# Loading the duplicated keys of an attention head with two 64-row transfers in place of one transfer with a repeat dimension

## The chip, the cores and the metric

The kernel runs on one core of a Trainium2 chip. The metric is device time in microseconds for one execution, the median of several. Five engines work side by side and meet at semaphores: TensorE (PE in the profile, with PEld for its weight loads), VectorE (DVE), ScalarE (ACT), GpSimd (POOL) and SyncE (SP). In this kernel every transfer is issued by SP, in program order, and carried out by the core's 16 DMA engines.

## What is computed

One inference step of a two-layer encoder over 1024 prompt positions and 8 x 16 sample positions (1152 rows of width 1024). Layer A has sliding-window attention with 16 heads on 4 key/value heads, layer B attention over the own chunk and 8 chunks back with 16 heads. After each attention come an output projection with layer norm and a GEGLU feed-forward part of width 2816 with a short causal convolution. Cut to what matters here:

```
h = x * (1 + sc_m) + sh_m
q, k, v = ...                                   # projections of h (layer B: k, v from the end of layer A)
s = einsum(q, k) * ATTN_SCALE + bias            # inside the band of chunks, else -1e30
p = softmax(s)                                  # layer A: with a learned sink per head
mix = (p @ v) @ w_o
x = layer_norm(ALPHA * x + (1 + g_m) * mix)
f = conv_ffn(x * (1 + sc_f) + sh_f)
x = layer_norm(ALPHA * x + (1 + g_f) * f)
```

All is float32. The kernel keeps that precision by writing each operand as the sum of two float32r numbers, a high part and a rest, and adding the products high x high, high x rest and rest x high.

## The kernel before

`attention(l, wk)` runs once for each layer (l is 0 and 1). First the keys and values are projected: `kproj` (L287) multiplies weights with the hidden rows `H` (through `mmT`, L266) and writes keys, split in high part and rest, to the DRAM tensor `kH[l]` (store on L299); `vproj` (L312, through `mmX`, L278) does the same for values into `vH[l]` (store on L328). Both take their staging tiles from a ring of four (`kvt`), so a tile's store must have landed before the fourth block after it can be written. In layer 1, `rescale` is woven in: for each of 9 row blocks it loads a block of `zd` (L893), multiplies and adds on POOL (L747, L748) and stores it to `xd` (L749), in a ring of two buffers.

Then 16 heads (8 pairs of channels c, two halves a) go through the prompt's attention. `kload(c, a)` brings a head's keys and values back into SBUF, into the tile `x1att`, with three transfers:

- `khi[a]` (L433), 128 partitions x 1024: the 64 rows of the high part of the keys, twice, in partitions 0 to 63 and again in 64 to 127. The query tile holds the query's high part in one half of the partitions and its rest in the other, so one matmul over 128 rows (L505) gives high x high and rest x high.
- `klo` (L434), 64 partitions x 1024: the rest of the keys, for the matmul on L510.
- `vst[a]` (L435), 128 partitions x 8 x 128: the values.

There are two of each tile for keys and values (a is 0 or 1). `kload` is called 4 times in layer 0 and 16 times in layer 1, 20 times in all: for the first pair before the head loop, for a later one as soon as a head's last block is through with the tile (in `finish`). Each head is worked in four pairs of query blocks: `scores` (bias load L484; matmuls; `softmax` with L471 on DVE and L475 on ACT), `weigh` (transposes L533, their split on L538 ACT and L539 DVE) and `values` (L552, ACT copy L564, store to `oT` on L567). Between them come the next pair's query projection (`qblock`, L266, ACT L457, DVE L458), the 16 work items of the sample rows (`item`, L601 to L681, one buffer for the cached values, L607), in layer 0 the modulation vectors (`ada`, weights loaded on L207, matmul L210), and at the end of the loop the loads and splits of the output projection's weights (L164, split on ACT L149 and POOL or DVE L160).

The order of the instructions on each engine is set when the program is built, by a scheduler that simulates times; at run time each engine works through its list in that order and waits at semaphores. SP's list is thus one line: a transfer that cannot be issued holds up all behind it, those of other tiles too.

Of the kernel before, what the change touches and what calls it, by code (L numbers as in the profile page):

```python
# [10 lines left out]
F32 = mybir.dt.float32  # L11
# [76 lines left out]
class Trunk:  # L88
# [249 lines left out]
    def attention(self, l, wk):  # L338
        nc, I = self.nc, self.I
# [6 lines left out]
        khi = [xa.take(1024) for _ in range(2)]  # L346
# [82 lines left out]
        def kload(c, a):  # L429
            r = slice(64 * a, 64 * a + 64)  # L430
            row = c * 128 + 64 * a
            kh, kl = kH[0, row : row + 64, :], kH[1, row : row + 64, :]
            nc.sync.dma_start(khi[a].bitcast(F32), bass.AP(kh.tensor, kh.offset, [[0, 2], [1024, 64], [1, 1024]]))  # L433
            nc.sync.dma_start(klo[r, :].bitcast(F32), kl)  # L434
            nc.sync.dma_start(  # L435
                vst[a].bitcast(F32), vH[:, 2 * c + a, :].rearrange("(k p) d -> p k d", p=128)
            )
# [258 lines left out]
        def finish(i):  # L696
            x = work[i]
            values(x)
            if x.g == 3:
                c, a = x.head.c, x.head.a  # L700
                if l == 1 and c < 7:
                    kload(c + 1, a)
                elif l == 0 and c == 3:
                    kload(1, a)
            if i == 6 * 8 - 1:
                sums(0)

        for a in range(2):
            kload(0, a)
# [639 lines left out]
```

## Time and profile before

| | |
|---|---|
| time, median of 3 runs (range) | 3238.45 us (3228.12 to 3243.93) |
| the profiled execution: its time, its span | 3225.61 us, 3223.7 us |
| granted TensorE clock, mean | 0.955 |
| key and value projection of layer 0, then its head loop | from about 55 to 117, 117 to 440 us |
| feed-forward part of layer 0 | 570 to 1480 us |
| key and value projection of layer 1, then its head loop | about 1555 to 1765, 1765 to 2190 us |
| output projection, feed-forward part of layer 1 | to 2370, to the end |

The profile is of one execution. In the rows of the timeline the first two numbers are the start and the time taken in microseconds, then come engine, line, operation and tiles; brackets at the end give how long the engine had been idle and what ended that. "SPq" rows are transfers being issued by SP: their time is that of the issuing alone, not of the transfer. In a table of windows the columns are the window, its length, the busy time of PE, PEld, DVE, ACT and POOL, the granted TensorE clock (1.00 is full speed), the mean busy share of the 16 DMA engines and the rate in GB/s.

### The profile page before, as it was taken

The page shows a single profiled execution, that of the slowest core. Times are in us where ns is not written, and L with a number is a line of the kernel's source. Part 1 is how long each engine was busy: PE and PEld are TensorE (multiplying, and loading weights), DVE is VectorE, ACT ScalarE, POOL GpSimd, SP SyncE. Part 2 cuts the span into 40 slices and gives each one's busy share as a digit, 9 for nine tenths or more (in the row PEclk, how much of TensorE's full clock was granted, in tenths as well). Part 3 has the DMA queues.
Part 4 walks back from the last instruction along what each step waited for, and adds up shares of the span by engine and source line. Part 5 has one row for each costly group of instructions (what it writes and reads, how often), then busy time and mean ns, then how long its engine had stood idle before and what let it go on. Part 6 is the DMA issues. An engine that isn't in the chain of part 4 may idle for free.

```text
span 3223.7 us, 42690 instructions
## 1 busy us (share of the span) xinstructions
PE 3004.9 (93%) x16524; PEld 2606.3 (81%) x16524; DVE 1519.0 (47%) x3162; ACT 1137.0 (35%) x2400; POOL 830.6 (26%) x599
## 2 busy tenths in 40 slices
PE   7799976999999999998899999987699999999996
PEld 4676755888888888897899877755589999999996
DVE  4244556724444443458213545545662444444458
ACT  3254632432222222224335555542244222222224
POOL 2001202422222222254451000000242222222243
PEclk8898987999999999999999999977899999999999
DMA  7334467532222222223685245458531111111122
GB/s 287 126 113 143 142 161 153 196 128 74 79 77 87 87 82 85 83 85 126 225 272 170 89 120 156 131 150 185 126 133 42 46 40 48 41 40 40 40 72 81
DMA packets 226035, 367.54 MB, mean 114 GB/s; under 512 B 34448, under 2 KB 148944, under 8 KB 225448
## 3 DMA queue, kind: packets, MB, share of 16 engines
q1 hardware_dynamic: 225832, 364.81, 36.6%
q8 instruction: 130, 2.13, 0.3%
q14 instruction: 73, 0.60, 0.1%
HBM read 289.40 MB, written 84.79 MB: 116 GB/s over the span
## 4 chain that ended last, share of the span: by engine, by line
PE 71%; DMA 12%; DVE 7%; SPq 3%; POOL 2%; issue 2%; ACT 2%; DVEq 0%; ACTq 0%; POOLq 0%
PE PS L266 41%; PE PS L1057 15%; PE PS L552 3%; PE PS L510 3%; PE PS L210 3%; PE PS L533 2%; PE PS L278 2%; PE PS L505 2%; DMA x1att<-rD 1%; DMA F<-rD 1%; DMA F<-zd 1%; DMA ws<-in_wo_dram 1%; DMA X<-oT 1%; DMA oT<-F 1%; DMA F<-xd 1%
## 5 line engine op out<-in xcount | busy, mean ns | idle before, releaser
L266 PE MATMUL PS<-H,wh 128*128 128x384 f32 (+1 forms) x5472 | 1057.8, 341 | 0.3 <-DVE H L160 0.3
L266 PEld LDWEIGHTS PS<-H,wh 128*128 128x128 f32 x5472 | 973.2, 190 | 20.6 <-issue 9.1
L266 PE MATMUL PS<-H,wl 128*128 128x384 f32 (+1 forms) x2736 | 576.3, 348 | 41.7 <-DVE X L327 13.5
L986 DVE SCALAR_TENSOR_TENSOR F<-PS,F 128x256 f32<-128x256 f32 (+2 forms) x704 | 353.0, 512 | 532.9 <-ACT F L983 519.5
L160 POOL TENSOR_TENSOR wl<-ws,wh 128x1024 fp32r<-128x1024 f32 x167 | 407.4, 2445 | 741.5 <-ACT wh L149 722.3
L266 PEld LDWEIGHTS PS<-H,wl 128*128 128x128 f32 x2736 | 493.4, 192 | 84.8 <-issue 37.5
L1057 PE MATMUL PS<-wh,X 128*128 128x512 f32 x1584 | 466.8, 394 | 12.8 <-DVE acc L1048 4.3
L983 ACT ACTIVATE F<-PS,F 128x384 f32<-128x384 f32 x264 | 177.4, 672 | 756.7 <-PE PS L266 755.3
L1057 PEld LDWEIGHTS PS<-wh,X 128*128 128x128 f32 x1584 | 294.2, 188 | 75.5 <-issue 9.2
L1048 DVE TENSOR_TENSOR acc<-acc,PS 128x512 f32<-128x512 f32 x324 | 221.5, 686 | 273.1 <-PE PS L1057 272.1
L1032 POOL TENSOR_TENSOR F<-F 128x384 f32<-128x384 f32 x132 | 138.1, 1046 | 642.5 <-ACT F L1030 640.6
L1057 PE MATMUL PS<-wl,X 128*128 128x512 f32 x792 | 246.8, 393 | 0.0
L278 PE MATMUL PS<-wh,H 128*128 128x256 f32 (+1 forms) x1008 | 198.8, 327 | 35.8 <-DVE H L160 27.7
L149 ACT CAST wh<-ws 128x1024 fp32r<-128x1024 f32 x176 | 182.1, 1045 | 132.5 <-PE PS L1057 76.9
L278 PEld LDWEIGHTS PS<-wh,H 128*128 128x128 f32 x1008 | 154.8, 199 | 51.7 <-DVE H L160 29.3
L1057 PEld LDWEIGHTS PS<-wl,X 128*128 128x128 f32 x792 | 149.3, 189 | 33.0
L160 DVE TENSOR_TENSOR X<-F,X 128x384 fp32r<-128x384 f32 x132 | 116.8, 885 | 101.6 <-ACT X L149 101.1
L533 PE MATMUL PS<-C,F 128*128 128x128 f32 x720 | 127.9, 294 | 14.2 <-DVE X L539 10.3
L471 DVE CUSTOM_DVE_ANT_0 F<-PS,F,C 128x256 f32<-128x256 f32 (+3 forms) x208 | 98.1, 481 | 80.7 <-PE PS L510 63.1
L485 POOL MEMSET F<- 64x64 f32 x32 | 4.6, 144 | 470.2 <-DMA F<-skb 250.9
L160 POOL TENSOR_TENSOR H<-F,H 128x1024 fp32r<-128x1024 f32 x23 | 58.4, 2537 | 248.2 <-ACT H L149 155.4
L471 DVE CUSTOM_DVE_ANT_0 F<-PS,F 128x320 f32<-128x320 f32 (+5 forms) x144 | 67.7, 481 | 109.2 <-PE PS L533 67.1
(192 smaller groups left out, 3310.2 us busy)
## 6 DMA issues: line engine op xcount, KB each, us to landing
ws<-in_wup_dram SPq DMA_DIRECT2D x88, 512.0 KB
F<-in_adaw_dram SPq DMA_DIRECT2D x74, 512.0 KB
ws<-in_wdn_dram SPq DMA_DIRECT2D x44, 512.0 KB
ws<-in_adaw_dram SPq DMA_DIRECT2D x32, 512.0 KB
X<-oT SPq DMA_DIRECT2D x64, 256.0 KB
xd<-F SPq DMA_DIRECT2D x27, 512.0 KB
F<-xd SPq DMA_DIRECT2D x27, 512.0 KB
x1att<-kH SPq DMA_DIRECT2D x20, 512.0 KB
```

Source lines behind the costliest of these rows:

```text
L149: nc.scalar.copy(out, in_)
L160: self.eng(el).tensor_sub(lo, src, hi.bitcast(F32))
L210: nc.tensor.matmul(ps[32 * j : 32 * j + 32, :], self.cT[:, k * 32 : k * 32 + 32], w[:, j2 * 512 : j2 * 512 + 512], start=k == 0, stop=k == ...
L266: self.nc.tensor.matmul(out[:, 0:n], w[a][:, k * 128 : k * 128 + 128], H[:, p, k, s0 : s0 + n], start=i == 0, stop=i == 23)
L278: self.nc.tensor.matmul(out[:, 0:n], H[:, p, j * kn + k, t0 : t0 + 128], w[a][:, k * n : k * n + n], start=i == 0, stop=i == 23,)
L471: nc.vector.tensor_tensor_reduce(out=p[:, c0 : c0 + w], in0=ps, in1=b, scale=1.0, scalar=init, op0=ALU.add, op1=ALU.min, accum_out=nm)
L533: nc.tensor.transpose(t[:, m * 128 : m * 128 + 128], p[:, (kt - k0) * 128 : (kt - k0) * 128 + 128], self.ident)
L983: nc.scalar.activation(y, ps[:, off : off + 384], AF.Identity, bias=w(3), scale=w(2))
L986: nc.vector.scalar_tensor_tensor(o, u, w(i), o, op0=ALU.mult, op1=ALU.add)
L1032: nc.gpsimd.tensor_mul(a, y, ya[bi])
L1048: nc.vector.tensor_add(row[:, n], row[:, n], ps)
L1057: nc.tensor.matmul(ps, ac[m][p][:, cs], w[m][q][:, n], start=i == 0, stop=i == 5)
```

## The change

The transfer of L433, whose source reads the same 64 rows twice through a leading dimension of size 2 and step 0, becomes two transfers, each of 64 rows to one half of the partitions, with no repeat in the source.

```diff
             kh, kl = kH[0, row : row + 64, :], kH[1, row : row + 64, :]
-            nc.sync.dma_start(khi[a].bitcast(F32), bass.AP(kh.tensor, kh.offset, [[0, 2], [1024, 64], [1, 1024]]))
+            for b in range(2):
+                nc.sync.dma_start(khi[a][64 * b : 64 * b + 64, :].bitcast(F32), kh)
             nc.sync.dma_start(klo[r, :].bitcast(F32), kl)
```

Lines behind it move by one: the changed kernel's two loads of `khi` are on L434, that of `klo` on L435, of the bias on L485. The same bytes are read and written. The lists of PE, DVE, ACT and POOL hold the same instructions in the same order as before (but for line numbers and buffer numbers); only SP's list changes, by 20 transfers more and by some exchanges near them.

SP's list at the first loads of layer 0, before (x1att_273 is layer 0's tile with `khi`, `klo` and `vst`; kH_78 and vH_82 are the DRAM tensors of keys and values):

```order
L433 DMA x1att_273<-kH_78 128x1x1024
L328 DMA vH_82<-X_70 128x512
L434 DMA x1att_273<-kH_78 64x1024
L433 DMA x1att_273<-kH_78 128x1x1024
L434 DMA x1att_273<-kH_78 64x1024
L328 DMA vH_82<-X_70 128x512
L484 DMA F<-ska 128x256
L207 DMA ws<-in_adaw_dram 128x1024 x2
L484 DMA F<-ska 128x256
L328 DMA vH_82<-X_70 128x512
```

The same place with the change, where L434 is `khi` and L435 `klo`:

```order
L434 DMA x1att_273<-kH_78 64x1024
L328 DMA vH_82<-X_70 128x512
L434 DMA x1att_273<-kH_78 64x1024
L435 DMA x1att_273<-kH_78 64x1024
L434 DMA x1att_273<-kH_78 64x1024
L328 DMA vH_82<-X_70 128x512
L434 DMA x1att_273<-kH_78 64x1024
L435 DMA x1att_273<-kH_78 64x1024
L485 DMA F<-ska 128x256
L207 DMA ws<-in_adaw_dram 128x1024
L328 DMA vH_82<-X_70 128x512
```

The second store of values now stands between the halves of the second `khi`, ahead of the second `klo`, and the third stands ahead of the second weight load of `ada`.

SP's list at the first loads of layer 1, in the key projection, before (x1att_10403 is layer 1's tile; xd_91 and zd are the store and the load of `rescale`):

```order
L433 DMA x1att_10403<-kH_79 128x1x1024
L434 DMA x1att_10403<-kH_79 64x1024
L433 DMA x1att_10403<-kH_79 128x1x1024
L299 DMA kH_79<-X_70 128x2x384
L749 DMA xd_91<-F 128x1024
L893 DMA F<-zd 128x1024
L434 DMA x1att_10403<-kH_79 64x1024
L164 DMA ws<-in_wk_dram 128x1024
L299 DMA kH_79<-X_70 128x2x384
```

And with the change:

```order
L434 DMA x1att_10407<-kH_79 64x1024 x2
L435 DMA x1att_10407<-kH_79 64x1024
L299 DMA kH_79<-X_70 128x2x384
L750 DMA xd_91<-F 128x1024
L894 DMA F<-zd 128x1024
L434 DMA x1att_10407<-kH_79 64x1024
L164 DMA ws<-in_wk_dram 128x1024
L434 DMA x1att_10407<-kH_79 64x1024
L299 DMA kH_79<-X_70 128x2x384
L306 DMA out_kb_dram<-F 128x256
L435 DMA x1att_10407<-kH_79 64x1024
```

The second head's `khi` now stands behind the key store and the `zd` load that it stood ahead of.

## The prediction

> **What bounds the kernel now.** I read the page first, then the shares of its chain, then the stages in which the changed loads stand.
>
> ```profile
> PE 3004.9 (93%) x16524; PEld 2606.3 (81%) x16524; DVE 1519.0 (47%) x3162; ACT 1137.0 (35%) x2400; POOL 830.6 (26%) x599
> PE 71%; DMA 12%; DVE 7%; SPq 3%; POOL 2%; issue 2%; ACT 2%; DVEq 0%; ACTq 0%; POOLq 0%
> ```
>
> PE is the bound on the whole, and its list is not touched. What can be gained is time in which PE stands still for a transfer, and time in which it runs on half a clock after standing still. So the question is how the loads of `khi` behave. From the table of windows, a stretch in which two such loads are the only large ones under way, and a stretch in which a `klo` load of 64 rows has joined one:
>
> ```profile
> 92.00:94.00 2.00, 2.00 (x19) 2.00 (x19) 0.00 (x0) 0.00 (x0) 0.00 (x0) 1.00 0.13 53
> 2128.00:2129.00 1.00, 1.00 (x7) 1.00 (x6) 0.00 (x0) 0.00 (x0) 1.00 (x1) 0.50 0.72 217
> ```
>
> The last two columns decide: 0.13 of 16 DMA engines is two of them, at 53 GB/s. A `khi` load moves 512 KB, so it takes 524288 / 53000 = 9.9 us, two in a row 20 us, with 14 engines idle. The dimension of size 2 in its source fits that number. The 64-row load of `klo` runs on nearly all: 217 GB/s, of which 217 - 53 = 164 are its own.
>
> A load that lasts is not yet a loss; SP's own rows show why it becomes one. These are issues of transfers behind a `khi` load:
>
> ```profile
> 84.92 0.53 SPq L433 DMA_DIRECT2D x1att<-kH  x1
> 85.49 8.84 SPq L434 DMA_DIRECT2D x1att<-kH  x1
> 94.44 0.74 SPq L328 DMA_DIRECT2D vH<-X  x1
> 1580.89 8.84 SPq L299 DMA_DIRECT2D kH<-X  x1
> 1899.80 10.47 SPq L567 DMA_DIRECT2D oT<-F  x1
> ```
>
> An issue is normally half a microsecond; here one takes 8.8 to 10.5 us, since a transfer that wants all 16 engines cannot be handed to the two that are full. SP works in order, so everything behind stands: the store of values at 94.44 could have followed 85.5.
>
> **Where PE pays.** Rows of PE with the idle time ahead of them, in order of time, then rows of ACT that stand behind four of these:
>
> ```profile
> 99.19 0.74 PE L278 MATMUL PS<-wh,H 128*128 128x256 f32 x4 [2.77 <-DVE X L327]
> 117.30 2.90 PE L266 MATMUL PS<-H,wl 128*128 128x384 f32 x8 [13.47 <-DVE X L327]
> 288.09 1.94 PE L210 MATMUL PS<-ws,C 128*32 128x512 f32 x8 [2.38 <-DMA ws<-in_adaw_dram]
> 1608.69 1.80 PE L266 MATMUL PS<-H,wl 128*128 128x384 f32 x5 [2.33 <-ACT F L305]
> 1662.66 1.65 PE L266 MATMUL PS<-H,wl 128*128 128x384 f32 x4 [6.29 <-DVE X L298]
> 1824.49 0.74 PE L552 MATMUL PS<-wl,x1att 128*128 128x256 f32 x4 [0.68 <-ACT F L564]
> 1917.49 1.22 PE L552 MATMUL PS<-X,x1att 128*128 128x256 f32 x4 [2.57 <-ACT F L564]
> 2073.84 1.66 PE L654 MATMUL PS<-F 128*32 128x128 f32 x24 [5.12 <-ACT F L564]
> 2113.67 1.54 PE L533 MATMUL PS<-C,F 128*128 128x128 f32 x6 [10.03 <-DVE X L539]
> ```
>
> ```profile
> 112.52 0.37 ACT L326 CAST X<-PS 128x256 fp32r<-128x256 f32 x1 [13.84 <-DMA vH<-X]
> 1607.16 0.48 ACT L297 CAST X<-PS 128x384 fp32r<-128x384 f32 x1 [16.89 <-DMA kH<-X]
> 1917.06 0.37 ACT L564 COPY F<-PS 128x256 f32<-128x256 f32 x1 [2.76 <-DMA oT<-F]
> 2071.83 1.04 ACT L149 CAST x1att<-ws 128x1024 fp32r<-128x1024 f32 x1 [9.12 <-DMA ws<-in_wo_dram]
> 2111.36 1.04 ACT L149 CAST x1att<-ws 128x1024 fp32r<-128x1024 f32 x1 [10.48 <-DMA ws<-in_wo_dram]
> ```
>
> PE names DVE or ACT, but these wait for a DMA: for a store that frees a staging tile, or for a weight that came late behind a `khi` load and held ACT's whole list at its cast. Each of these nine comes within 33 us of a `khi` load's issue, save 1662.66, whose link is the chain of waits below.
>
> After such gaps the granted clock falls to a half. The windows, and a row at full clock to set beside that of 117.30:
>
> ```profile
> 100.20:103.60 3.40, 3.40 (x18) 3.38 (x17) 0.00 (x0) 0.00 (x0) 0.00 (x0) 0.50 0.87 239
> 117.30:120.70 3.40, 3.40 (x11) 3.40 (x12) 0.60 (x2) 0.74 (x2) 0.00 (x0) 0.50 0.67 247
> 287.90:298.20 10.30, 10.11 (x50) 7.59 (x51) 2.89 (x9) 2.78 (x7) 2.00 (x1) 0.50 0.48 167
> 1608.90:1612.30 3.40, 3.40 (x12) 3.40 (x12) 0.00 (x0) 0.00 (x0) 2.65 (x2) 0.50 0.63 204
> 1660.10:1666.90 6.80, 4.24 (x13) 4.24 (x14) 0.56 (x1) 5.43 (x15) 0.00 (x0) 0.50 0.80 282
> 1916.10:1929.80 13.70, 12.31 (x44) 9.16 (x45) 4.74 (x18) 5.56 (x14) 0.29 (x2) 0.50 0.39 112
> 2073.10:2083.40 10.30, 9.56 (x50) 6.92 (x51) 5.31 (x12) 5.35 (x14) 2.26 (x1) 0.50 0.32 118
> 2107.30:2144.80 37.50, 31.13 (x153) 21.49 (x154) 14.46 (x50) 14.61 (x36) 2.66 (x3) 0.50 0.47 136
> 123.10 1.55 PE L266 MATMUL PS<-H,wl 128*128 128x384 f32 x8
> ```
>
> Eight matmuls took 2.90 us against 1.55, a factor of 1.87: of each busy microsecond at half clock, 1 - 1/1.87 = 0.47 is lost.
>
> **The change, term by term.** It removes 20 loads of about 9.9 us on two engines and puts 40 of 64 rows in their place. Such a half, 262144 bytes, takes 1.2 us at 217 GB/s and 1.6 us at 164, so a head's `khi` takes 2.4 to 3.2 us, and leaves no two full engines behind it. What goes with them is part of each stall above; by stage:
>
> 1. *Values of layer 0 (80 to 121 us).* Idle 2.77 + 13.47 = 16.2; half clock 0.47 x (3.40 + 3.40) = 3.2. At most 19.4. The stores keep a neighbour in two whole key loads, bias and weights, so some waiting can stay: I take 15.
> 2. *Head loop of layer 0.* Idle 2.38, half clock 0.47 x 10.11 = 4.8, at most 7.1. The late weight was issued right behind a `khi` load, but another half-clock window precedes it without one: I take 4.
> 3. *Keys of layer 1.* Idle 2.33 + 6.29, half clock 0.47 x (3.40 + 4.24) = 3.6, at most 12.2. The second gap hangs on the `rescale` chain, which starts late; from the chain of waits:
>
> ```profile
> 1592.01 17.50 DMA F<-zd
> 1618.94 3.95 DMA F<-zd
> ```
>
> The first load of `zd` behind the `khi` loads takes 17.5 us, a later one 4; the 13.5 us move all of the chain ahead. I take 9, since POOL also paces it.
> 4. *Head loop of layer 1.* Idle 0.68 + 2.57 + 5.12 + 10.03 = 18.4; half clock 0.47 x (12.31 + 9.56 + 31.13) = 24.9; at most 43.3. Behind the gap at 2113.67 stand other large loads still (bias, the output weights, caches: some 1.6 MB within 6 us of 2092.59, 8 us at 200 GB/s), so I keep 2 or 3 us of it, and that the clock falls there in part. I take 32, the least sure of the terms.
>
> What is added is SP's time:
>
> ```profile
> L433 SPq DMA_DIRECT2D x1att<-kH x20: 517/522/823, 82.9 to 2126.1; - x20
> SPq L164 <- DMA ws<-in_wdn_dram: 25.2, 19, 3.4
> ```
>
> Twenty more issues of 0.52 us, 10 us in all, spread over 20 places where SP today loses up to 10 us at once. Behind each half stand `klo`, the bias and the `oT` stores; a delay of 0.5 us is below what their buffers hide. If it were not hidden it would cost these 10 us. The second row is the sort of wait that one more transfer in flight can bring SP: 1.3 us on average when it waits for an earlier transfer to land. The exchanges in SP's list cost nothing that I can see: the second head's `khi` of layer 1 is wanted only some 200 us later, and the third store of values of layer 0 comes earlier by one load.
>
> Sum: 15 + 4 + 9 + 32 = 60. The profiled execution's 3225.61 (span 3223.7 and 1.9 around it) becomes 3166. It lies 12.8 below the median of the three runs; from that median I forecast 3238.45 - 60 = **3178 us**.
>
> **A rule that speaks against the change.** The Trainium skill, page "SBUF — State Buffer", section "Can I just issue two DMAs to hit both halves?", says no: two transfers to the two halves of the partitions run one behind the other, and 64 rows have about the bandwidth of 32 (196 GB/s in its table). The trace agrees on the rate of a 64-row load, 164 to 217 GB/s. By the page's figure, 512 KB one behind the other is an estimated 2.7 us, which leaves the sum as it is: serial halves on all engines still beat 53 GB/s. If one read the rule as "two halves bring nothing over one transfer", the time would be that of the third rival.
>
> **Rivals.**
> - *All of it goes:* the clock stays up at every one of these places. 19.4 + 7.1 + 12.2 + 43.3 = 82, 3156. For it: the gaps have one cause. Against it: the half-clock windows are many and one of 37.5 us follows a gap of 10.
> - *Hidden in part:* the weight loads at 2060 and 2100 are late anyway through the other bulk, and the staging stores of layer 0 through bias and weights. Then the terms give 9 + 2 + 5 + 9 = 25, 3213. For it: at 250 GB/s the other loads there fill much of the window.
> - *It doesn't do what it says:* the halves land no sooner than one load does today, and SP has only more to issue. Then 3238 to 3249. Against it: the `klo` row.
> - *Slower:* SP's list becomes the bound. Each of the 20 added issues costs 0.52 us and one wait of 1.3 us for an earlier landing, with `oT` stores behind it, and ACT and PE behind these: 20 x 1.8 = 37, 3275. It decides from the point where the halves together take longer than the 9.9 us of today, since until then SP is freed of more than it is given. Against it: the same row.
>
> **Chances.** Forecast 0.62, all of it 0.13, hidden in part 0.15, no effect 0.06, slower 0.04. The range goes from the profiled execution's own 3225.61 less all 82 (3144) to the case of partial hiding: 3145 to 3214. A measurement can tell about 0.5% (16 us) from no change. Faster by more: 0.89; within it: 0.07; slower: 0.04.
>
> **What would show it.** In the profile after: no window of 0.13 with 53 GB/s after a `khi` load; no issue of 8 us on SP behind one (term 1, 3 and 4); PE's gaps at 99, 117, 1608 and 1662 gone, and the first `zd` load near 4 us; the casts of the output weights (L149) waiting under 3 us; a clock above 0.955. I am wrong if the 64-row halves show 0.13 again, if the gaps stay with other loads as releasers, or if the half-clock windows stay where the gaps have gone.

## The result, and the profile after

The changed kernel takes 3144.14 us (median of 4 runs, 3140.24 to 3149.55); the kernel before, timed beside it, takes 3235.7 (median of 4, 3228.12 to 3243.93). The ratio is 0.9718, with a 95% interval of 0.9687 to 0.9748: faster, by 91.6 us at the medians. The profiled execution of the changed kernel takes 3140.24 us (span 3138.1), that of before 3225.61, a difference of 85.4. The prediction was 3178, with a range down to 3145: the direction and the cause were right, the gain was half as large again as forecast, and the time lies 0.9 us below the range.

First the page of the changed kernel: the engines' busy time, and the shares of the chain that ended last.

```profile
PE 2964.6 (94%) x16524; PEld 2576.5 (82%) x16524; DVE 1523.4 (49%) x3162; ACT 1137.7 (36%) x2400; POOL 832.7 (27%) x599
PE 79%; DMA 7%; DVE 7%; ACT 2%; issue 2%; POOL 2%; SPq 1%; DVEq 0%; ACTq 0%; POOLq 0%
```

PE has the same 16524 matmuls and is busy for 40 us less: the same work at a higher clock (0.971 on the mean against 0.955). The rest of the 85 us is standing still that went. In the chain, the shares of DMA and of SP's issuing fell from 12% and 3% to 7% and 1%.

Next SP's rows of the changed kernel around the second load of `khi` in layer 0, and two rows that group all loads of `khi` (L434) and `klo` (L435): number, shortest, median and longest issue in ns, first and last start in us.

```profile
86.93 0.59 SPq L434 DMA_DIRECT2D x1att<-kH  x1
87.64 0.52 SPq L328 DMA_DIRECT2D vH<-X  x1
88.20 0.44 SPq L434 DMA_DIRECT2D x1att<-kH  x1
88.69 0.60 SPq L435 DMA_DIRECT2D x1att<-kH  x1
```

```profile
L434 SPq DMA_DIRECT2D x1att<-kH x40: 444/492/1088, 84.3 to 2050.0; - x40
L435 SPq DMA_DIRECT2D x1att<-kH x20: 450/547/597, 86.3 to 2050.7; - x20
```

The store of values between the loads is issued in half a microsecond, as is the `klo` load behind them; before, the `klo` load behind the second `khi` took 8.84. The windows of the changed kernel say why. The first stands among the loads of keys (three halves and a `klo` load have been issued, and two stores of values), the second at the two microseconds that the prediction showed of before. The other five hold the matmuls behind the gaps of before at 99 and 117, at 1608 and 1662, at 1917, at 2073 and at 2113 us, which had run on half a clock and now start earlier (by 1.4 us at the first gap, by 73 at the last):

```profile
86.00:88.00 2.00, 2.00 (x19) 2.00 (x19) 0.00 (x0) 0.37 (x1) 0.00 (x0) 1.00 0.86 246
92.00:94.00 2.00, 2.00 (x19) 2.00 (x19) 0.00 (x0) 0.00 (x0) 0.00 (x0) 1.00 1.02 251
84.00:104.00 20.00, 20.00 (x160) 20.00 (x159) 2.46 (x6) 2.57 (x8) 0.58 (x4) 1.00 0.92 269
1560.00:1640.00 80.00, 80.00 (x484) 80.00 (x483) 9.99 (x20) 24.81 (x54) 48.94 (x21) 1.00 0.88 292
1868.70:1876.00 7.30, 7.30 (x46) 5.52 (x46) 5.84 (x21) 5.08 (x13) 0.00 (x0) 1.00 0.31 86
2014.70:2020.30 5.60, 5.60 (x52) 4.16 (x52) 3.21 (x9) 2.85 (x6) 0.00 (x0) 1.00 0.53 180
2041.00:2062.00 21.00, 20.36 (x168) 14.43 (x168) 14.23 (x50) 12.59 (x33) 2.38 (x1) 1.00 0.77 217
```

Between 92 and 94 us, where the kernel before moved 53 GB/s on a share of 0.13, the changed one moves 251 on all 16 engines, loads and stores together. In all five places the clock is 1.00.

Then PE's waits between 1765 and 2110 us in the changed kernel (total us, times, longest). In this stage, which ran to 2145 us, the kernel before waited 18.4 us in the four gaps of term 4:

```profile
PE PS L534 <- DVE C L677: 1.5, 1, 1.5
PE PS L655 <- ACT F L476: 1.5, 2, 1.1
```

These are the two largest, and neither stands behind a transfer. Between 80 and 121 us PE has no wait at all.

Since PE executes the same list in both kernels, the start of the same matmul in the two traces tells what had been saved up to there. The differences, by stretches of the time before:

| stretch (us of before) | in the prediction | saved, us | bound | taken |
|---|---|---|---|---|
| 80 to 130 | term 1 | 19.8 | 19.4 | 15 |
| 130 to 440 | term 2 | 8.8 | 7.1 | 4 |
| 1555 to 1765 | term 3 | 12.4 | 12.2 | 9 |
| 1765 to 2145 | term 4 | 44.5 | 43.3 | 32 |
| all else | none | -0.3 | 0 | 0 |
| sum | | 85.2 | 82 | 60 |

Each term came out at its upper bound or a little above. So two questions are for experiments. Is it the width of the transfer that counts, or its splitting and the other order of SP's list? And does the lost clock go with the gap, at one place and with one load?

### The profile page after: what moved, and what is told of

The parts are those of the page before. It is cut to its first block, busy times and chain, and to the rows that moved or that the text cites. A ratio compares the mean times of both kernels' runs of the same rounds, so it can differ in the third digit from the quotient of the medians.

```text
span 3138.1 us, 42714 instructions
## 1 busy us (share of the span) xinstructions
PE 2964.6 (94%) x16524; PEld 2576.5 (82%) x16524; DVE 1523.4 (49%) x3162; ACT 1137.7 (36%) x2400; POOL 832.7 (27%) x599
## 4 chain that ended last, share of the span: by engine, by line
PE 79%; DMA 7%; DVE 7%; ACT 2%; issue 2%; POOL 2%; SPq 1%; DVEq 0%; ACTq 0%; POOLq 0%
PE PS L266 45%; PE PS L1058 15%; PE PS L278 4%; PE PS L553 3%; PE PS L511 3%; PE PS L534 3%; PE PS L210 3%; PE PS L506 2%; DMA X<-oT 1%; DMA x1att<-rD 1%; DMA F<-xd 1%; DMA F<-in_xrow_dram 1%; PE PS L655 1%; DVE F L948 1%; DMA F<-rD 1%
## 5 line engine op out<-in xcount | busy, mean ns | idle before, releaser
L266 PEld LDWEIGHTS PS<-H,wh 128*128 128x128 f32 x5472 | 966.3, 188 | 20.8 <-issue 9.1
L266 PE MATMUL PS<-H,wl 128*128 128x384 f32 (+1 forms) x2736 | 567.5, 344 | 17.9 <-DVE H L151 11.3
L266 PEld LDWEIGHTS PS<-H,wl 128*128 128x128 f32 x2736 | 486.8, 189 | 60.4 <-issue 22.0
L1031 ACT ACTIVATE F<-F 128x384 f32<-128x384 f32 x132 | 69.2, 524 | 139.7 <-DVE F L987 126.1
L278 PE MATMUL PS<-x1att,H 128*128 128x512 f32 x432 | 113.6, 409 | 4.4 <-ACT x1att L149 4.3
```

The lines of the kernel that those rows point to most:

```text
L266: self.nc.tensor.matmul(out[:, 0:n], w[a][:, k * 128 : k * 128 + 128], H[:, p, k, s0 : s0 + n], start=i == 0, stop=i == 23)
L278: self.nc.tensor.matmul(out[:, 0:n], H[:, p, j * kn + k, t0 : t0 + 128], w[a][:, k * n : k * n + n], start=i == 0, stop=i == 23,)
```

## The experiments

**The same two transfers, but narrow.** The first theory (width): what cost time is that a source with a leading dimension of 2 runs on two of the 16 DMA engines. Its rival (list): two transfers of 64 rows and the exchanges in SP's list are what helps. Three kernels have the changed kernel's list on every engine, SP's included, but write the source of each half so that its leading dimension is 2, 4 or 8. The edit for 4, against the kernel before (for 2 and 8 alike, with `[[1024, 2], [2 * 1024, 32], [1, 1024]]` and `[[1024, 8], [8 * 1024, 8], [1, 1024]]`):

```diff
-            nc.sync.dma_start(khi[a].bitcast(F32), bass.AP(kh.tensor, kh.offset, [[0, 2], [1024, 64], [1, 1024]]))
+            hs = bass.AP(kh.tensor, kh.offset, [[1024, 4], [4 * 1024, 16], [1, 1024]])
+            for b in range(2):
+                nc.sync.dma_start(khi[a][64 * b : 64 * b + 64, :].bitcast(F32), hs)
```

For a leading 2:

> Two loads of 64 rows to each half as in the changed kernel, but the source is walked as 2 groups of 32 rows (even rows, then odd rows), so its leading dimension is 2 (the keys' rows come in another order, so the attention is not the reference's). SP's list and those of all engines are those of the changed kernel. Theory 'width' (a load runs on as many DMA engines as its leading dimension lets it): the 13% share and 50 GB/s come back, issues of 8 us on SP come back, the time is that of before, 3225 to 3250 us. Rival 'list' (the gain is from one transfer cut into two and from the exchanges in SP's list): 3140 to 3155 us, as the changed kernel.

For a leading 4:

> As halves_k2 with a leading dimension of 4 (4 groups of 16 rows; rows in another order). 'Width': 4 engines, a share of 25% and about 105 GB/s while only keys are loaded, 5 us for a head's keys; half to three quarters of the gain, 3160 to 3195 us. 'List': as the changed kernel, 3140 to 3155 us.

For a leading 8:

> As halves_k2 with a leading dimension of 8 (8 groups of 8 rows; rows in another order). 'Width': 8 engines, about 210 GB/s, which is what a load to 64 partitions reached on 16 (164 to 217 GB/s), so nearly all of the gain, 3142 to 3160 us. 'List': 3140 to 3155 us.

A fourth kernel keeps one transfer of 128 partitions, but without a repeat: its 128 rows are all different ones.

```diff
-            nc.sync.dma_start(khi[a].bitcast(F32), bass.AP(kh.tensor, kh.offset, [[0, 2], [1024, 64], [1, 1024]]))
+            nc.sync.dma_start(khi[a].bitcast(F32), kH[0, c * 128 : c * 128 + 128, :])
```

> One transfer, as in the kernel before, but of 128 different rows (those of the pair of heads) with no repeat dimension, so half of the duplicated keys are another head's and the attention is not the reference's; the bytes are the same. 'Width': 16 engines, all of the gain, and 20 issues on SP fewer than the changed kernel: 3135 to 3150 us. 'List': one transfer as before, so the time of before, 3225 to 3250 us.

Measured, beside the kernel before at 3232.91 on the same chip:

| source of `khi` | median, us (range) | ratio, 95% interval |
|---|---|---|
| two halves, leading 2 | 3222.91 (3212.18 to 3227.57) | 0.9959 (0.9932 to 0.9985) |
| two halves, leading 4 | 3191.66 (3185.72 to 3205.83) | 0.987 (0.9814 to 0.9927) |
| two halves, leading 8 | 3148.59 (3146.61 to 3171.03) | 0.9747 (0.9687 to 0.9806) |
| one transfer of 128 rows, no repeat | 3140.9 (3135.99 to 3153.96) | 0.9713 (0.9659 to 0.9768) |

The list of the changed kernel with narrow halves gives the old time less 10 us; one transfer with a wide source gives the new one. The list of this last kernel differs from that of before only in five transfers that have changed places. Width decides, and the rival falls as the cause of the 90 us. The leading 2 came out 2 us below its expected band: the splitting or the order of the list may have brought about 10 us at the medians (5 to 22 by the interval). No run here tells these two apart.

The profile of the kernel with a leading 2: SP's row for all of its `khi` loads, two of its issues, two windows, and the largest waits of PE in the changed stages.

```profile
L435 SPq DMA_DIRECT2D x1att<-kH x40: 484/518/5175, 82.3 to 2122.6; - x40
```

```profile
85.99 5.17 SPq L435 DMA_DIRECT2D x1att<-kH  x1
91.21 4.69 SPq L436 DMA_DIRECT2D x1att<-kH  x1
```

```profile
90.00:92.00 2.00, 2.00 (x19) 2.00 (x19) 0.00 (x0) 0.00 (x0) 0.00 (x0) 1.00 0.13 53
92.00:94.00 2.00, 2.00 (x19) 2.00 (x18) 0.42 (x1) 0.37 (x1) 0.00 (x0) 1.00 0.13 51
```

```profile
PE PS L266 <- DVE X L327: 17.1, 1, 17.1
...
PE PS L535 <- DVE X L541: 10.7, 1, 10.7
```

Everything of the kernel before is there again: 53 GB/s, issues of about 5 us (a half moves half the bytes), the gap behind the staging of values (17.1 us, before 13.47) and that at the transposes near the end (10.7, before 10.03).

The kernel with a leading 4 shows, in layer 0, that a slow load can cost without a long issue. First the group of its `khi` loads, then the waits of PE and, between 60 and 140 us, of ACT:

```profile
L435 SPq DMA_DIRECT2D x1att<-kH x40: 509/537/607, 81.4 to 2100.3; - x40
```

```profile
PE PS L266 <- DVE X L327: 7.7, 1, 7.7
```

```profile
ACT X L326 <- DMA vH<-X: 14.4, 3, 6.3
```

The longest issue of its `khi` loads is 0.61 us, against 5.17 with a leading 2, and of all that SP issues between 80 and 105 us nothing takes over 1.32 us. Yet ACT waits up to 6.3 us for a store of values to land, PE 7.7 us behind it, and of the 19.8 us of the stretch from 80 to 130 this kernel saves 10.0 by the same matmuls. Two steps of the chain that ends in PE's gap (start, us), the wait of SP between them, and ACT's cast behind the same store in the changed kernel show how:

```profile
82.88 11.43 DMA x1att<-kH
94.38 10.41 DMA vH<-X
SPq L328 <- DMA x1att<-kH: 4.3, 1, 4.3
98.53 0.65 ACT L326 CAST X<-PS 128x256 fp32r<-128x256 f32 x2 [3.99 <-DMA vH<-X]
```

A half that was issued at 82.88 lands 11.4 us later; SP waits 4.3 us for that landing before it issues the store, and the store, itself issued in 0.32 us, takes 10.4 us more to land. In the changed kernel the store was issued at 91.23, and the cast that waits for it starts 7.3 us later. So a long issue, which the prediction made the link between a slow load and a late transfer, is not the only link: SP also waits for a slow load to land, and a transfer that is issued quickly can still land late. In layer 1 these are not apart (a store to `oT` behind the last `khi` load takes 4.22 us to issue). A share of four engines, where 0.25 and 105 GB/s were expected, stands for instance behind the two halves issued at 1858.71:

```profile
1868.00:1870.00 2.00, 2.00 (x14) 1.97 (x13) 0.08 (x1) 0.00 (x0) 0.00 (x0) 1.00 0.26 93
```

The profiled execution of this kernel is the slowest of its four, so its rows show the kind of wait, and the medians the size: about half of the gain. With a leading 8 the median is within 8 us of the one wide transfer's. Its profiled execution, the slowest of its four too (3171.03), still has a wait of PE behind the staging of values, and saves 14.1 of the 19.8 us of that stretch:

```profile
PE PS L266 <- DVE X L327: 4.0, 1, 4.0
```

**One layer at a time.** Theory: the terms are independent and add up. Rival: a gain of layer 0 is waited away later, or the other way round. Each kernel has the new loads in one layer alone; here layer 0 (`if l == 1` for the other).

```diff
-            for b in range(2):
-                nc.sync.dma_start(khi[a][64 * b : 64 * b + 64, :].bitcast(F32), kh)
+            if l == 0:
+                for b in range(2):
+                    nc.sync.dma_start(khi[a][64 * b : 64 * b + 64, :].bitcast(F32), kh)
+            else:
+                nc.sync.dma_start(khi[a].bitcast(F32), bass.AP(kh.tensor, kh.offset, [[0, 2], [1024, 64], [1, 1024]]))
```

Layer 0 alone:

> The change in layer 0 alone (4 of the 20 loads), layer 1 as before. If the stages add up as the two traces lie (19.8 us saved up to 130 us and 8.8 in the rest of layer 0's attention), 3235.7 - 28.6 = 3207 us. Rival: savings of layer 0 are given back later (weights not yet there at the start of the feed-forward part): 3225 us and more.

Layer 1 alone:

> The change in layer 1 alone (16 of the 20 loads). If the stages add up, 12.5 us in the key projection and 44.5 in the head loop: 3235.7 - 57 = 3179 us. Rival: part of the later savings needed the earlier ones: 3190 us and more.

Beside them the changed kernel once more, on the same chip:

> The changed kernel again on the chip that runs the three above, as their measure: 3140 to 3150 us if chips agree.

Measured, beside the kernel before at 3241.34: layer 0 alone 3197.77 us, ratio 0.9888 (0.9842 to 0.9934); layer 1 alone 3172.14, ratio 0.9813 (0.9757 to 0.987); both 3144.33, ratio 0.9734 (0.9677 to 0.9791). 1.1% and 1.9% make 3.0%, against 2.7% for both, inside the intervals. The same matmuls in the profiles, compared with before, show it more sharply:

| stretch (us of before) | layer 0 alone | layer 1 alone | both, again |
|---|---|---|---|
| 80 to 130 | 19.8 | 0.3 | 19.8 |
| 130 to 440 | 8.9 | -0.1 | 12.5 |
| 1555 to 1660 | 0.8 | 10.7 | 10.7 |
| 1765 to 2095 | -2.5 | 20.8 | 19.8 |
| 2095 to 2145 | 0.0 | 22.4 | 22.5 |

Every stage has its gain from its own loads, to within a few microseconds, and none is waited away. How far a stretch moves with no changed load in it is a measure of the noise: up to 4.1 us (between 440 and 1555 us with layer 0 alone). The two gaps that the prediction named most are still there where the old loads are, PE's waits in layer 1's head loop of the first kernel and in layer 0's values of the second:

```profile
PE PS L537 <- DVE X L543: 10.0, 1, 10.0
```

```profile
PE PS L266 <- DVE X L327: 12.8, 1, 12.8
```

**One old load alone.** The largest single gap, before at 2113.67, was put down to the output weights coming late behind the last pair's `khi` load. This kernel is the changed one with that single load (pair 7, half 0, layer 1) in the old form. The theories differ in what it brings back: the gap and the clock ("one load, one gap"), the gap alone ("clock apart"), or nothing, if the 1.6 MB of other loads there fill the time anyway ("bulk").

```diff
-            for b in range(2):
-                nc.sync.dma_start(khi[a][64 * b : 64 * b + 64, :].bitcast(F32), kh)
+            if l == 0 or c < 7 or a == 1:
+                for b in range(2):
+                    nc.sync.dma_start(khi[a][64 * b : 64 * b + 64, :].bitcast(F32), kh)
+            else:
+                nc.sync.dma_start(khi[a].bitcast(F32), bass.AP(kh.tensor, kh.offset, [[0, 2], [1024, 64], [1, 1024]]))
```

> The changed kernel with one of its 20 loads in the old form, that for the first head of the last pair in layer 1. Theory 'one load, one gap': the cast of the output weights waits some 10 us again, PE stands 10 us, and the clock stays at a half for 30 us or more behind it: 10 + 12 to 15 of half clock = 20 to 26 us, 3164 to 3172 us. Rival 'clock apart': the gap of 10 us comes back but not the long half clock: 3150 to 3156 us. Rival 'bulk': with the other two-engine loads gone, one more is hidden: 3141 to 3148 us.

It takes 3157.56 us (3154.92 to 3168.51), ratio 0.9774 (0.9718 to 0.9829), 13.2 us over the changed kernel beside it: between the first two theories. Its intervals overlap with the changed kernel's, so the profile has to decide. PE's row, ACT's row, the window behind them, and SP's row of the old load and of what stood behind it:

```profile
2050.60 1.54 PE L537 MATMUL PS<-C,F 128*128 128x128 f32 x6 [10.22 <-DVE X L543]
```

```profile
2048.29 1.04 ACT L149 CAST x1att<-ws 128x1024 fp32r<-128x1024 f32 x1 [10.66 <-DMA ws<-in_wo_dram]
```

```profile
2045.20:2065.70 20.50, 15.10 (x75) 10.61 (x75) 7.93 (x26) 8.57 (x20) 2.20 (x3) 0.50 0.42 121
```

```profile
2029.33 0.57 SPq L437 DMA_DIRECT2D x1att<-kH  x1
...
2032.20 0.34 SPq L164 DMA_DIRECT2D ws<-in_wo_dram  x1
2034.75 0.38 SPq L605 DMA_DIRECT2D F<-in_ckB_dram  x1
2035.23 5.04 SPq L571 DMA_DIRECT2D oT<-F  x1
```

One load brings the whole gap back (10.22 us; 10.03 before), and a half-clock stretch of 20.5 us with it, where before had 37.5. By the factor of the prediction this stretch costs 0.47 x 15.10 = 7.1, with the gap 17.3. The same matmuls say 15.9: between 2095 and 2145 us this kernel saves 6.6, the changed one 22.5. "Bulk" falls, and so does "clock apart", since a half-clock stretch came back with the gap; of "one load, one gap" the expected size was too large, 30 us or more where 20.5 came. Note the weight: it was issued at 2032.20, in 0.34 us, and ACT could start its cast 16 us later. That is again the late landing, not a long issue.

## Why the prediction was right, and where it failed

**The mechanism held.** No window of 0.13 is left behind a `khi` load, no issue of 8 us stands behind one, the gaps at 99, 117, 1608 and 1662 us are gone, and the clock is above 0.955. Of the nine gaps whose rows the prediction showed, each stage's went with that stage's loads, as the kernels with one layer show. The Trainium skill, page "DMA: Bandwidth & Descriptors", section "Rules for kernel authors", says that an outermost dimension smaller than 16, a leading broadcast for one, keeps a transfer on at most that many engines; the trace agrees, with a share of 0.13 (two of 16) both for the repeat of before and for a leading 2 without a repeat. The prediction's reason for the long issues, that the two engines are full, fits the kernel with a leading 2: at the same share its issues take 5.17 and 4.69 us with 256 KB under way in place of 512. How much the engines take before an issue stands, no run shows.

**The rule weighed against the change** ("Can I just issue two DMAs to hit both halves?") did not decide. One transfer of 128 rows and two of 64 differ by 3.2 us at the medians (3140.9 and 3144.14, from different sets of runs), less than either interval, so two halves bring nothing over one wide transfer. The Trainium skill, page "SBUF — State Buffer", in the section of that name, says that only one transfer spanning all 128 partitions reaches all of the memory's ports for DMA; the runs agree as far as the halves gain nothing over such a transfer. But the one transfer that they replaced here was not wide.

**What is added cost nothing measurable.** The kernel with one wide transfer has none of the 20 added issues and other exchanges in SP's list, and is faster by the same 3.2 us at the medians, which the intervals do not tell from nothing. The rivals "slower" and "it doesn't do what it says" fall.

**The step that failed is the sizing of the terms,** the "I take 15", "4", "9" and "32" under bounds of 19.4, 7.1, 12.2 and 43.3. They measured 19.8, 8.8, 12.4 and 44.5, so the rival "all of it goes" (82) is what happened. One by one:

1. Term 1 kept 4 us since the stores still have whole key loads, bias and weights beside them. That waiting is there, for ACT, which stands before the cast in `vproj` between 60 and 140 us of the changed kernel:

```profile
ACT X L326 <- DMA vH<-X: 11.0, 3, 4.4
```

It was 13.84 us at the longest before. But 4.4 us on ACT no longer reaches PE, which has no wait there. The discount was taken on the wrong engine: a gap on PE is what is left of ACT's wait above PE's lead, and it goes to zero before the wait does.

2. Term 2 kept 3 us since a half-clock window stood there without a `khi` load. It gave 8.8, and 8.6 to 12.5 in the profiles of layer 0 alone, of the single old load and of the changed kernel again. The reading of that window was wrong. It begins 2.5 us after the issue of the `khi` load at 268.44, and PE waits in it for a late weight, as it does at 288.09; of before:

```profile
273.66 1.92 PE L210 MATMUL PS<-ws,C 128*32 128x512 f32 x4 [1.35 <-DMA ws<-in_adaw_dram]
270.90:277.70 6.80, 5.45 (x21) 2.98 (x19) 1.19 (x6) 3.02 (x9) 2.34 (x1) 0.50 0.65 202
```

With this gap and its half clock (1.35 + 0.47 x 5.45 = 3.9) the bound is 11.0, and between 270 and 300 us of before the same matmuls save 11.1. The wait and the window go with the new loads in layer 0 alone, and stay with those in layer 1 alone. Short half-clock stretches elsewhere in the stage of the changed kernel (3.4 us each at 306.9 and 361.5) take part of it back.

3. Term 3 kept 3 us since "POOL also paces" the `rescale` chain. POOL's wait for `zd` between 1540 and 1700 us, of the changed kernel, then of before:

```profile
POOL F L748 <- DMA F<-zd: 16.5, 7, 4.4
```

```profile
POOL F L747 <- DMA F<-zd: 30.2, 7, 20.1
```

The total fell by 13.7, close to the 13.5 that the chain of waits had given, and the stage gave 12.4. PE has no wait left between 1540 and 1700 us: POOL's own work was no limit.

4. Term 4 is 12.5 of the 25 that were missing. It rested on the words that a part of the gap at 2113.67 would stay, as other loads of 1.6 MB need 8 us, "and that the clock falls there in part". The estimate of the landing was right. Of the changed kernel, SP's last `khi` issue and the weight's, and the cast that needs it:

```profile
2029.41 1.09 SPq L434 DMA_DIRECT2D x1att<-kH  x2
...
2032.26 0.34 SPq L164 DMA_DIRECT2D ws<-in_wo_dram  x1
```

```profile
2038.25 1.05 ACT L149 CAST x1att<-ws 128x1024 fp32r<-128x1024 f32 x1 [0.54 <-DMA ws<-in_wo_dram]
```

The weight is there 8.8 us after the `khi` issue, but ACT has come to this cast only half a microsecond earlier, and PE loses nothing. What failed is to have kept 2 or 3 us of a gap without setting the landing time beside the time at which ACT would ask; and to have kept most of the lost clock (some 8 us) for so short a gap. With no gap the clock stayed at 1.00 (the window at 2041 above).

**The rest of the miss.** Forecast and result are 34 us apart. The terms are 25 of it. Another 6 is that the medians differ by 91.6 and the profiled executions by 85.4, and 3 that the median of before moved from 3238.45 to 3235.7: the spread of executions. The range had left nothing for it, since its lower end was the profiled execution less 82; by the prediction's own working that is 3144 (3143.6), and it was written as 3145.

## What to carry to other kernels

Look at the leading dimension of a transfer's source when the windows show a fixed small share of the DMA engines: here 2 gave 0.13 and 53 GB/s, and the price was paid by the transfers around it. When several gaps on the bound engine have one cause, forecast that all of them go, the lost clock too, unless a row shows that the next releaser comes later than the engine will ask; a wait that stays on another engine is by itself no reason for a discount, as the first term shows. And a range that is built on one profiled execution must have the spread of executions added.

## What the runs showed of the hardware beyond this

- The time falls with the width up to 8, not in one step: 3223, 3192 and 3149 us for leading dimensions of 2, 4 and 8, and 3141 for one wide transfer on the same chip. At 8 nearly all of the gain is there by the median, with an interval of 63 to 101 us.
- A narrow load hurts in more than one way. At 2 it holds up the issues behind it (5.17 us for a 256 KB half, 8.84 behind the 512 KB load). At 4, in layer 0, no issue is held so, but SP waits up to 4.3 us for a half to land, and a transfer behind it lands late (10.4 us for a store, where the changed kernel's took 7.3): half of that stage's gain is lost. In all a leading 4 costs 51 us against the one wide transfer beside it. Why the store lands late stays open.
- A gap of 10 us on PE, at the same matmuls, brought half-clock stretches of different length: 37.5 us in the kernel before (gap 10.03) and with layer 0 alone (9.97), 27.3 with a leading 2 (10.71), 20.5 with the single old load (10.22). All half-clock stretches in the rows shown, from 3.4 to 37.5 us, are whole multiples of 3.4 us. What sets the length stays open. Layer 0 alone, then the leading 2:

```profile
2075.40:2112.90 37.50, 31.26 (x153) 21.60 (x154) 14.62 (x50) 14.75 (x37) 2.66 (x3) 0.50 0.48 139
2102.50:2129.80 27.30, 20.21 (x94) 14.64 (x95) 10.97 (x39) 10.90 (x27) 2.66 (x3) 0.50 0.41 118
```
